# A hybrid mixer kernel: modulation products on TensorE, loads queued later, and other places for stores, gathers and mLSTM fetches

## The chip, the cores and the metric

The kernel runs on one core of a Trainium2 chip. The metric is the device time of one execution in microseconds (us); lower is better. The engines are named as in the profile: PE (TensorE, with PEld for its weight loads), DVE (VectorE), ACT (ScalarE), POOL (GpSimd) and SP, which here only issues DMAs. Each engine works through its own queue in the order of the program.

## The reference

The program computes two transformer blocks over 512 tokens of width 1024, all in float32. The change touches the first half of the first block, the mixer, and the adaptive modulation beside it:

```python
mod = c_act @ ada_w + ada_b                          # one row of 6 x 1024, from silu(c)
hn = rmsnorm(x) * (1 + sc1) + sh1
proj = hn @ w_in                                     # 1024 -> 6208 columns
a_qkv, a_z, a_gates, b_qk, b_v, b_o, b_gates, merge = split(proj)
# branch a: gated delta rule, 8 heads, chunks of 64 tokens, both directions
sol = triangular_solve(lower + I, [v*beta, k*beta*exp(g)])
for c in chunks:  v_new = u_c - w_c @ S;  S = S * cd + kd_c.T @ v_new
# branch b: mLSTM, 8 heads, both directions, weights exp(log_d - m)
y = sigmoid(gate_a) * (o_a @ w_branch_a) + sigmoid(gate_b) * (h_b @ w_branch_b)
x = x + gt1 * (y @ w_out)
```

Behind it come a mixture of 32 experts, and a second block, run as two layers of attention and feed-forward. Each of the three modulations (`ada0`, `ada1`, `ada2`) is one row vector times a 1024 x 6144 matrix, and each weight is used once.

## The kernel before

Activations lie feature-major, 128 features by 512 tokens a tile, split into a high and a low part (`hi`, `lo`), so that a product of weights and activations is three matmuls (`mm3`): high by high, high by low, low by high. Weights come as *units*. A raw block of 1024 x 256 (1 MB, tile `raw`, four buffers) is loaded over the SP queue (`_load`); each unit takes half of it, ACT rounds it to `whi` (L196), POOL subtracts to get `wlo` (L205), and 24 matmuls into a PSUM bank `pd` follow. A unit of the token-major kind (`tm`) does the same with the operands swapped.

The order is written by hand. `unit` first calls `_ahead`, which issues the splits of the next two units; `_loads` issues a new load whenever fewer than four raw blocks are held. Before the change `_loads` also runs after each split in `_ahead` and in `done` for a block used unsplit. This order decides what stands behind what on the queue of SP, which issues the loads of weights, the stores of projected tiles (`later`, one tile behind), the gathers of the delta rule and the reloads.

The modulation unit (`ada`, L457) takes a raw block of 1024 x 256 whole: ACT multiplies four of its eight 128-row slices by `c` in place, DVE multiplies and adds the other four into `adacc`, POOL adds the four of ACT and then the two sums, and two matmuls against a column of ones (`pa<-ones,adacc`) add up the 128 partitions. 24 such units run inside the mixer, 16 more in the first attention layer, 24 in the first feed-forward part (there on DVE alone). The opening of the kernel has another form, `ada_first`: eight matmuls `pada<-wa,crep`, each with 32 equal weight columns, four of them side by side on the array, and then two against `wmean`.

In the mixer two generators run against each other. The main one is the delta rule for four heads (`gdn`, twice) and then the mLSTM; the other, `fill`, is the projection of w_in (`gdn_proj`, `spill_tm`, `spill_fm`), with a modulation unit woven in after every 8.4 credits of work (two pieces at 4.2 each), and the branch product `branch_a` behind it. `drive` takes from `fill` as many credits as the main generator yields; a tile of `pd` is 5.2 credits. So the yields set how much projection is placed between two steps of the delta rule, on every queue.

In `gdn` the steps that matter here are, in order: products `pG`, `M` and `E` on DVE; `M` stored to DRAM (`md`, ACT's queue) and gathered back as `L` by eight DMAs on SP; `Rk` and `kd` on DVE; 31 steps of forward substitution on DVE (`stmp<-L,Tm`, `Tm<-Tm,stmp`), the *solver*; results to DRAM (`yd`, `xd`) and gathered back as `Xc` and `Y` by twelve DMAs; then `pQ`, `pY`, `pw`, `pu`, and a scan over eight chunks (`pv`, `pS`, each answered by DVE).

In the mLSTM a step (head pair f, key block a) needs a tile `rowt`, read from DRAM (`mdram`) and spread over 128 partitions (ACT's queue), masked by POOL (L1399), raised to exp by ACT (`weights`), multiplied on DVE with the scores `pqk`, and used in the matmuls `pm`. After four steps `mlstm_out` normalises, gates with `og` (loaded there, on SP) and transposes (`pht`).

Of the kernel before, what the change touches and what calls it, by code (L numbers as in the profile page):

```python
# [21 lines left out]
P = 128  # L22
# [153 lines left out]
class Build:  # L176
    def __init__(self, tc, I, O, order=None):
        self.tc, self.nc, self.I, self.O = tc, tc.nc, I, O
        self.orders_in = order
        self.orders = {}  # L180
        self.curset = None
        self.uid = 0
        self.lead_ps = {}
        self.pending = None
# [143 lines left out]
    def unit(self, key, sel):  # L328

        i = len(self.order)  # L330
# [27 lines left out]
    def _ahead(self, i):  # L358
        self._loads()
        while self.nsplit < len(self.order_in) and sum(s[0] != "raw" for _, s in self.order_in[i + 1:self.nsplit + 1]) <= self.w_ahead:  # L360
# [12 lines left out]
            self._loads()  # L373
# [83 lines left out]
    def ada(self, w, c, bias, out, groups, eng=None):  # L457
# [3 lines left out]
        for g in groups:  # L461
# [31 lines left out]
            self.tt(out[:, s], ps[:, 0:16], bias[:, s], OP.add)  # L493

# [425 lines left out]
    def gdn_proj(self, g, cv=None, dram=None):  # L920

        for c in range(3):
# [52 lines left out]
    def gdn(self, g, mx, qk, v, Y, Tm, z_d, o_d, side=None, decay=None):  # L975
# [52 lines left out]
        for d in range(2):  # L1028
            for half in range(2):
                for par in range(2):  # L1030
                    p0 = 64 * d + 32 * half + 16 * par
                    s0 = 64 * par + 32 * half
                    dst = (Lr if d == 0 else Lt)[p0:p0 + 16]
                    self.dma("sync", dst, md[s0:s0 + 32, d, :, 32 * half:32 * half + 32].rearrange("r q c -> q r c"))
# [8 lines left out]
        for d in range(2):  # L1043
# [3 lines left out]
            yield 5.0  # L1047
        nc.vector.tensor_copy(Lt[0:64], Lr[0:64, ::-1, ::-1])
        tmp = mx.tile([P, 256], F32, tag="stmp", name="stmp")
        for j in range(31):  # L1050
# [5 lines left out]
            if j % 4 == 3:  # L1056
                yield 2.6
# [190 lines left out]
        yield 5.0  # L1248
        for f in range(2):
# [128 lines left out]
    def mlstm(self, mp, qk, v_d, o_d, oh, ol):  # L1378
# [5 lines left out]
        rowt = {}  # L1384

        def fetch(i):
            if i < len(steps):
                f, a = steps[i]
                t = rowt[i] = mp.tile([P, 2, 640], F32, tag="rowt", bufs=5, name="rowt")
                self.dma("scalar", t, self.mdram[2 * f:2 * f + 2, a, :].partition_broadcast(P))  # L1390

        def weights(i):
            if i < len(steps):
                f, a = steps[i]
                t, n = rowt[i], T - P * a
                for d in range(2):
                    dg = t[:, :, T:] if d else t[:, :, 0:P]
                    sg = -1 if d else 1
                    nc.gpsimd.affine_select(dg, dg, pattern=[[0, 2], [sg, P]], compare_op=OP.is_ge, fill=NEG, base=0, channel_multiplier=-sg)  # L1399
                for hh in range(2):  # L1400
                    for d, r in ((0, t[:, hh, 0:n]), (1, t[:, hh, n:])):
# [1403 lines left out]
```

## Time and profile before

| | |
|---|---|
| median of 3 runs | 2731.18 us (2724.32 to 2737.99) |
| the profiled execution | 2728.39 us, its span 2726.6 us |
| PE busy over the span | 2490.4 us (91%) |
| DVE, ACT, POOL busy | 1524.1, 929.5, 957.9 us |
| granted clock of PE, mean | 0.952 of full speed |
| opening | 0 to 62 us |
| gates and the first projection | 62 to 110 us |
| delta rule, heads 0 to 3, and heads 4 to 7 | 110 to 305, and 305 to 484 us |
| mLSTM | 484 to 632 us |
| merge, output product | 632 to about 790 us |

The stages are told from the tiles: `E` of the first group starts at 110 us, the transposes of the second begin at 329, `va` is loaded at 486.5, `pht` of the last head pair ends at 632. In the later stages (expert mixture, two layers) PE is busy nearly throughout. The chain of work that ended last begins at 1103 us and so says nothing of the mixer; there the waits of PE, taken by stage, are read instead. A granted clock between two levels (1.2 and 2.4 GHz, 0.5 and 1.0 in the rows) is a mean over a stretch.

### The profile page before, as it was taken

The numbers are of one execution on the slowest core, as the hardware profiler recorded it, in microseconds if no ns is written. First come the engines' busy times: TensorE is split into PE (matmuls) and PEld (weight loads), VectorE is DVE, ScalarE is ACT, GpSimd is POOL, SyncE is SP. The second block draws the span as 40 slices with busy tenths as digits, with TensorE's granted clock in tenths as the row PEclk, the third lists the DMA queues.
The fourth block names the chain that finished last, engine by engine and source line by source line (L and its number), as shares of the span: only waits on it lengthen the run. The fifth ranks groups of instructions, "written<-read, shape, count | busy, mean of one in ns | idle before, by whom it ended". The sixth has DMA issues, their size and how long they took to land.

```text
span 2726.6 us, 35040 instructions
## 1 busy us (share of the span) xinstructions
PE 2490.4 (91%) x13618; PEld 1843.4 (68%) x13618; DVE 1524.1 (56%) x2483; ACT 929.5 (34%) x1534; POOL 957.9 (35%) x652
## 2 busy tenths in 40 slices
PE   7888888787969999889999999999999999999999
PEld 4676776566634444557777877878757777888887
DVE  4896595354446645564455488884454345452523
ACT  3434233444222211333444432323332344442432
POOL 1454454332320000443553333444332343344443
PEclk8989898788979999999999999999999999999999
DMA  9356465534389974432446146552331225232321
GB/s 264 93 187 180 150 183 179 203 108 136 102 325 357 391 301 146 135 124 93 146 148 201 63 154 201 170 192 89 102 93 47 85 82 189 78 108 80 106 93 62
DMA packets 332299, 419.07 MB, mean 154 GB/s; under 512 B 33608, under 2 KB 275760, under 8 KB 323680
## 3 DMA queue, kind: packets, MB, share of 16 engines
q1 hardware_dynamic: 312848, 377.12, 41.8%
q10 hardware_dynamic: 14624, 25.28, 2.7%
q0 software_dynamic: 4656, 14.35, 1.6%
q8 instruction: 113, 1.85, 0.3%
q14 instruction: 58, 0.48, 0.1%
HBM read 387.66 MB, written 33.23 MB: 154 GB/s over the span
## 4 chain that ended last, share of the span: by engine, by line
PE 45%; DVE 6%; issue 3%; POOL 2%; ACT 2%; DMA 1%; ACTq 0%; POOLq 0%; DVEq 0%
PE pd L199 36%; PE psc L199 2%; DVE adacc L214 2%; PE tm L199 2%; POOL wlo L205 2%; PE ptot L199 1%; DMA raw<-in_w_up 1%; DVE cv L214 1%; PE po L199 1%; DVE h L214 1%; PE prr L199 1%; PE pc L199 1%; PE pz L199 1%; PE pso L199 1%; PE pst L199 1%
## 5 line engine op out<-in xcount | busy, mean ns | idle before, releaser
L205 POOL TENSOR_TENSOR wlo<-raw,whi 128x1024 fp32r<-128x1024 f32 (+3 forms) x317 | 720.6, 2279 | 1219.3 <-ACT whi L196 1069.6
L199 PE MATMUL pd<-h,whi 128*128 128x512 f32 (+1 forms) x3440 | 1098.6, 401 | 32.9 <-DVE stg L214 6.3
L199 PEld LDWEIGHTS pd<-h,whi 128*128 128x128 f32 x3440 | 646.4, 193 | 191.0 <-issue 27.1
L199 PE MATMUL pd<-h,wlo 128*128 128x512 f32 (+1 forms) x1720 | 675.9, 393 | 21.9 <-POOL wlo L205 21.9
L196 ACT ACTIVATE whi<-raw 128x1024 fp32r<-128x1024 f32 (+3 forms) x319 | 313.9, 993 | 260.4 <-PE pd L199 117.2
L199 PEld LDWEIGHTS pd<-h,wlo 128*128 128x128 f32 x1720 | 331.4, 193 | 94.4 <-POOL wlo L205 26.2
L199 PE MATMUL pd<-fyh,whi 128*128 128x512 f32 (+1 forms) x546 | 204.7, 375 | 9.3 <-ACT whi L196 5.3
L214 DVE SCALAR_TENSOR_TENSOR cv<-pd,vec,cv 128x511 f32<-128x511 f32 (+1 forms) x176 | 131.8, 749 | 143.8 <-ACT cv L196 138.3
L199 PE MATMUL pd<-fyh,wlo 128*128 128x512 f32 (+1 forms) x546 | 201.8, 370 | 5.5 <-POOL wlo L205 5.5
L214 DVE SCALAR_TENSOR_TENSOR adacc<-raw,cs,adacc 128x256 f32<-128x256 f32 x288 | 201.5, 700 | 9.4
L199 PE MATMUL pd<-fyl,whi 128*128 128x512 f32 (+1 forms) x546 | 200.8, 368 | 0.2 <-DVE fyl L205 0.2
L214 DVE SCALAR_TENSOR_TENSOR xTl<-pd,mod,xTl 128x512 f32<-128x512 f32 (+1 forms) x73 | 49.4, 683 | 188.5 <-PE pd L199 188.5
L199 PE MATMUL pgB<-gu,xt 128*64 128x512 f32 (+1 forms) x304 | 143.1, 608 | 0.3 <-PEq L1981 0.3
L199 PE MATMUL pgA<-gu,xt 128*64 128x512 f32 (+1 forms) x304 | 143.2, 608 | 0.0
L199 PE MATMUL tm<-whi,h 128*128 128x256 f32 x640 | 130.7, 297 | 8.3 <-ACT whi L196 7.9
L199 PEld LDWEIGHTS pd<-fyh,whi 128*128 128x128 f32 x546 | 104.6, 192 | 40.1 <-ACT whi L196 10.4
L199 PEld LDWEIGHTS pd<-fyh,wlo 128*128 128x128 f32 x546 | 104.4, 191 | 24.3 <-POOL wlo L205 7.5
L199 PEld LDWEIGHTS pd<-fyl,whi 128*128 128x128 f32 x546 | 104.7, 192 | 16.8 <-DVE fyl L205 0.7
L199 PEld LDWEIGHTS tm<-whi,h 128*128 128x128 f32 x640 | 107.2, 200 | 9.6 <-ACT whi L196 8.2
L199 PE MATMUL tm<-wlo,h 128*128 128x256 f32 x320 | 93.9, 293 | 7.7 <-POOL wlo L205 7.6
L196 ACT ACTIVATE cv<-pd,vec 128x512 f32<-128x512 f32 x88 | 68.2, 775 | 94.5 <-PE pd L199 93.9
L214 DVE SCALAR_TENSOR_TENSOR xT<-pb,mod,xT 128x512 f32<-128x512 f32 x128 | 87.0, 742 | 2.1 <-PE pb L199 1.9
(564 smaller groups left out, 3366.9 us busy)
## 6 DMA issues: line engine op xcount, KB each, us to landing
raw<-in_ada SPq DMA_DIRECT2D x64, 1024.0 KB, 5.4
raw<-in_w_in SPq DMA_DIRECT2D x54, 1024.0 KB, 6.7
raw<-in_w_up SPq DMA_DIRECT2D x44, 1024.0 KB, 4.9
gu<-in_wg SPq DMA_DIRECT2D x30, 1024.0 KB, 8.7
gu<-in_wu SPq DMA_DIRECT2D x30, 1024.0 KB, 7.0
dn<-in_wd SPq DMA_DIRECT2D x59, 512.0 KB, 9.7
raw<-in_w_dn SPq DMA_DIRECT2D x16, 1024.0 KB, 5.1
raw<-in_wo SPq DMA_DIRECT2D x12, 1024.0 KB
```

What stands on the lines that cost most here:

```text
L196: return self.nc.scalar.activation(out, in_, func, **kw)
L199: return self.nc.tensor.matmul(out, lhsT, rhs, start=start, stop=stop)
L205: return (eng or self.nc.vector).tensor_tensor(out, a, b, op=op)
L214: return (eng or self.nc.vector).scalar_tensor_tensor(out, a, s, b, op0=op0, op1=op1)
```

## The change

1. **Modulation products.** The 24 units inside the mixer use a new generator `ada_mm`: eight matmuls `pada<-raw,cs` on the raw block, with a column of `c` repeated 32 times as weights, in four column groups; ACT copies the result to `adacc`; two matmuls against `wmean` one unit later. DVE's, ACT's and POOL's passes over the block go. A unit yields 1.2 credits, where the old one yielded none, and comes after every 6.0 credits. The units of the later stages stay as they are.
2. **Later loads.** `_loads` is called at the head of `_ahead` alone, no longer after a split or in `done`. This holds for the whole program.
3. **Stores.** `later` keeps two tiles back, not one; `gdn` flushes them before its last transposes.
4. **Delta rule.** The eight gathers of `L` are issued after the first `Rk`, `kd` and a yield, no longer before them. The solver yields 3.9 credits every four steps, not 2.6. The projection of z comes before the last third of the second `gdn_proj`.
5. **mLSTM.** `rowt` is fetched on SP, four steps ahead instead of three, with the first (and every sixth) in a buffer of its own. The first one is fetched, masked and raised to exp inside the scan of the second `gdn`. `og` is loaded one step before it is used, into two buffers. `oa` is no longer loaded whole on ACT's queue: `branch_in` loads its quarters on SP, two at the start of the mLSTM and two when the first are split.

```diff
     def _ahead(self, i):
...
             self.nsplit += 1
-            self._loads()
...
     def done(self, u):
...
                 del self.raws[key]
-                self._loads()
...
+    def ada_mm(self, w, c, bias, out, groups):
+        for g in groups:
+            pcol = self.ps.tile([P, T], F32, tag="a", bufs=self.ps_a, name="pa")
+            pend = None
+            for j in range(9):
+                if j < 8:
+                    u = self.unit((w, 0, KD, 2048 * g + 256 * j, 256), ("raw",))
+                    ps = self.pc("pada")
+                    for k in range(KD):
+                        q = 32 * (k % 4)
+                        self.mm(ps[q:q + 32, 0:256], c[:, k:k + 1].to_broadcast([P, 32]), u[1][:, k, :], k < 4, k >= 4)
+                    self.done(u)
+                if pend is not None:
+                    for i in range(2):
+                        self.mm(pcol[:, 2 * j - 2 + i:2 * j - 1 + i], pend[:, i * P:(i + 1) * P], self.wmean)
+                if j < 8:
+                    pend = self.gp.tile([P, 256], F32, tag="adacc", bufs=2, name="adacc")
+                    self.act(pend, ps[:, 0:256], AF.Copy)
+                    yield 1.2
...
             self.tt(Tm[:, j + 1:, 0:w], Tm[:, j + 1:, 0:w], tv, OP.subtract)
             if j % 4 == 3:
-                yield 2.6
+                yield 3.9
...
+    def mlstm_fetch(self, t, f, a):
+        self.dma("sync", t, self.mdram[2 * f:2 * f + 2, a, :].partition_broadcast(P))
...
-            fetch(i + 3)
+            fetch(i + 4)
             weights(i + 2)
...
+                if a == 2:
+                    og[f] = mp.tile([P, 4, P], F32, tag="og", bufs=2, name="og")
+                    self.dma("sync", og[f], o_d[:, :, P * f:P * f + P])
...
     def later(self, out=None, in_=None):
...
+        if out is not None:
+            self.pending.append((out, in_))
+        while len(self.pending) > (2 if out is not None else 0):
+            self.dma("sync", *self.pending.pop(0))
...
-        ada = self.chain(ada0((1, 2)), self.ada("ada1", c2, self.vc("ada_b1"), mod1, (0,), nc.gpsimd))
+        ada = self.chain(self.ada_mm("ada0", c1, self.vc("ada_b0"), mod0, (1, 2)), self.ada_mm("ada1", c2, self.vc("ada_b1"), mod1, (0,)))
...
-                    self.gdn_proj(1, None, cv_d), self.mark("g1"), self.spill_tm("w_in", 1536, 2, z_d),
+                    self.gdn_proj(1, None, cv_d, (0, 1)), self.spill_tm("w_in", 1536, 2, z_d), self.gdn_proj(1, None, cv_d, (2,)), self.mark("g1"),
```

What stands in a row on PE at the first modulation units, in the first delta group. Before, a unit shows there only as the two matmuls against ones:

```order
L199 MATMUL pd<-h_95,wlo 128x512
L199 MATMUL pG<-gqk_472 64x64 x32
L199 MATMUL pa<-ones,adacc 128x1 x2
L199 MATMUL pd<-h_96,whi 128x512
L199 MATMUL pd<-h_104,whi 128x512
L199 MATMUL pd<-h_96,wlo 128x512
```

After, with the same names (`pl` is the norm of the heads, `cs` the column of c):

```order
L199 MATMUL pl_923<-sq,const_gmask 128x512
L199 MATMUL pada<-raw,cs_146 32x256 x8
L199 MATMUL pa<-wmean,adacc 128x1 x2
L199 MATMUL pd<-h_98,whi 128x512
L199 MATMUL pd<-h_106,whi 128x512
L199 MATMUL pd<-h_98,wlo 128x512
```

Eight matmuls have come in between two projection steps; the two that follow belong to the unit before.

On POOL from the clearing of `Tm` to the end of the first solver, before (the group of three `wlo` is the one that PE waits for at 198 us):

```order
L1039 MEMSET Tm 128x32
L205 TENSOR_TENSOR raw<-raw 128x512
L205 TENSOR_TENSOR adacc<-adacc,raw 128x256 x2
L205 TENSOR_TENSOR wlo<-raw,whi 128x1024 x3
L205 TENSOR_TENSOR raw<-raw 128x512
L205 TENSOR_TENSOR adacc<-adacc,raw 128x256 x2
L205 TENSOR_TENSOR wlo<-raw,whi 128x1024
```

and after, from the same clearing to the scan:

```order
L1053 MEMSET Tm 128x1024
L1054 MEMSET Tm 128x32
L205 TENSOR_TENSOR wlo<-raw,whi 128x1024 x10
L1178 MEMSET S 128x256
L205 TENSOR_TENSOR zg<-zg,rows 128x1024
```

The additions of the modulation have left POOL's queue; only the subtractions for `wlo` are left in this stretch.

On SP at the start of the mLSTM, before (`rowt` and `oa` are on ACT's queue there):

```order
L217 DMA raw<-in_w_in 128x8x256
L217 DMA raw<-in_wa 128x4x256
L217 DMA va<-v_d 128x520 x4
L217 DMA row_ml_g<-in_rows 128x512
L217 DMA mg_d<-stg 128x512
```

and after, from the reload of the mLSTM's q and k in the scan on:

```order
L217 DMA mqk_4038<-qk_d 128x512 x2
L217 DMA rowt<-mdram 128x2x640
L217 DMA mg_d<-stg 128x512 x2
L217 DMA raw<-in_wa 128x4x256
L217 DMA mg_d<-stg 128x512 x3
L217 DMA raw<-in_wa 128x4x256
L217 DMA va<-v_d 128x520
L217 DMA rowt<-mdram 128x2x640
L217 DMA va<-v_d 128x520
L217 DMA rowt<-mdram 128x2x640
```

The first `rowt` has moved ahead of the loads of `wa` and `va`, into the scan, and the next ones alternate with `va` on the same queue.

## Rows read from the trace of the kernel before

**Rows 1.** Busy time by stretch (start:end, length, each engine, clock, DMA share, GB/s)
```profile
110.00:484.00 374.00, 307.35 (x3548) 258.00 (x3548) 273.09 (x444) 135.88 (x225) 176.72 (x121) 0.91 0.56 170
140.00:225.00 85.00, 65.42 (x543) 56.91 (x540) 81.23 (x128) 23.77 (x41) 44.70 (x30) 0.88 0.57 169
343.00:412.00 69.00, 56.65 (x288) 47.83 (x286) 65.93 (x101) 20.07 (x34) 35.82 (x25) 0.95 0.64 183
484.00:632.00 148.00, 112.92 (x545) 83.60 (x544) 63.82 (x156) 69.72 (x143) 47.10 (x59) 0.79 0.44 146
```

**Rows 2.** Waits of PE, 110 to 484 us: us in total, times, longest
```profile
PE pd L199 <- POOL wlo L205: 9.2, 1, 9.2
PE pl L199 <- ACT sq L196: 8.5, 2, 5.1
PE tm L199 <- ACT whi L196: 7.9, 2, 6.8
PE tm L199 <- POOL wlo L205: 7.6, 4, 2.0
PE pd L199 <- DVE stg L214: 6.3, 1, 6.3
...
PE pd L199 <- DVE stmp L205: 3.4, 1, 3.4
```

**Rows 3.** Groups by form, 110 to 570 us: count, busy us, mean ns, idle before
```profile
L214 DVE SCALAR_TENSOR_TENSOR adacc<-raw,cs,adacc 128x256 f32<-128x256 f32 x72 | 48.9, 679 | 2.6
L196 ACT ACTIVATE raw<-raw,cs 128x256 f32<-128x256 f32 x96 | 40.7, 495 | 3.8 <-DVE adacc L210 3.8
L205 POOL TENSOR_TENSOR adacc<-adacc,raw 128x256 f32<-128x256 f32 x48 | 40.0, 833 | 54.6 <-DVE adacc L214 51.7
L205 POOL TENSOR_TENSOR raw<-raw 128x512 f32<-128x512 f32 x24 | 34.7, 1445 | 2.1 <-ACT raw L196 2.1
```

**Rows 4.** PE in order of time, opening: start, us, what (two records a matmul)
```profile
43.17 1.92 PE L199 MATMUL pada<-wa,crep 128*32 128x256 f32 x16
...
47.76 1.07 PE L199 MATMUL pada<-wa,crep 128*32 128x256 f32 x16
48.76 0.61 PE L199 MATMUL pa<-wmean,adacc 128*128 128x1 f32 x4
```

**Rows 5.** POOL in order of time, end of the first solver
```profile
193.77 1.56 POOL L205 TENSOR_TENSOR adacc<-adacc,raw 128x256 f32<-128x256 f32 x2 [11.26 <-DVE adacc L214]
195.29 4.96 POOL L205 TENSOR_TENSOR wlo<-raw,whi 128x1024 fp32r<-128x1024 f32 x2
```

**Rows 6.** Start of the mLSTM: ACT's DMA queue, POOL, PE and ACT in order of time
```profile
492.48 1.51 ACTq L217 DMA_DIRECT2D rowt<-mdram  x3
500.84 0.77 POOL L1399 TENSOR_SCALAR_AFFINE_SELECT rowt<-rowt 128x256 f32<-128x256 f32 x2 [14.99 <-DMA rowt<-mdram]
502.98 1.33 PE L199 MATMUL pm<-va,rowt 128*128 128x65 f32 x5 [13.30 <-DVE rowt L214]
531.63 0.63 ACT L196 ACTIVATE oe<-og 128x512 f32<-128x512 f32 x1 [5.21 <-DMA og<-o_d]
```

**Rows 7.** Waits of PE, 484 to 632 us
```profile
PE pqk L199 <- DVE rowt L214: 9.3, 3, 3.7
PE pht L202 <- DVE hs L205: 6.2, 1, 6.2
```

**Rows 8.** SP's queue and DVE at the first solver, in order of time
```profile
146.19 5.43 SPq L217 DMA_DIRECT2D L<-md  x8
166.12 0.68 DVE L1048 COPY L<-L 64x1024 f32<-64x1024 f32 x1
```

**Rows 9.** Waits of PE, 1100 to 2726 us
```profile
PE pd L199 <- POOL wlo L205: 16.2, 12, 2.0
```

**Rows 10.** Waits of SP's queue, 110 to 632 us; a load's time to landing
```profile
SPq L217 <- POOL adacc L205: 88.7, 17, 16.4
raw<-in_ada SPq DMA_DIRECT2D x64, 1024.0 KB, 5.4
```

More of the change, by code (lines that the diff above doesn't have):

```diff
@@ L917, in gates, with gdn_proj @@
         yield 1.0
-    def gdn_proj(self, g, cv=None, dram=None):
-        for c in range(3):
+    def gdn_proj(self, g, cv=None, dram=None, parts=range(3)):
+        for c in parts:
             for j in range(2):
@@ L1047, in gdn @@
             yield 5.0
+            for dd in range(2 if d == 0 else 0):
+                for half in range(2):
+                    for par in range(2):
+                        p0 = 64 * dd + 32 * half + 16 * par
+                        s0 = 64 * par + 32 * half
+                        dst = (Lr if dd == 0 else Lt)[p0:p0 + 16]
+                        self.dma("sync", dst, md[s0:s0 + 32, dd, :, 32 * half:32 * half + 32].rearrange("r q c -> q r c"))
         nc.vector.tensor_copy(Lt[0:64], Lr[0:64, ::-1, ::-1])
@@ L1248, in gdn @@
         yield 5.0
+        self.later()
         for f in range(2):
@@ L1409, in mlstm @@
         self.mlg = self.big_row(mp, "ml_g")
-        for i in range(2):
-            weights(i)
-        out = None
+        weights(1)
+        out, og = None, {}
         for i in range(len(steps) + 1):
@@ L1516, in gate_loads, with branch_in, fetch @@
         return get
-    def branch_in(self, oa, hi, lo):
+    def branch_in(self, src, hi, lo, fill):
+        ts = []
+        def fetch(k):
+            if k < 4:
+                ts.append(self.gp.tile([P, T], F32, tag="mt", bufs=2, name="oat"))
+                self.dma("sync", ts[k], src[:, k])
+        for k in range(2):
+            fetch(k)
+        yield from fill
         for k in range(4):
-            self.split(oa[:, k], hi[:, k], lo[:, k])
+            self.split(ts[k], hi[:, k], lo[:, k])
+            fetch(k + 2)
         yield 0.0
@@ L2650, in pre2 @@
                         yield from self.mlstm_pre(g1["ml"], qk_d)
+                        g1["first"] = mb.tile([P, 2, 640], F32, tag="rowt0", name="rowt")
+                        self.mlstm_fetch(g1["first"], 0, 0)
+                        yield 0.0
+                        yield 0.0
+                        self.mlstm_weights(g1["first"], 0, 0)
                     sh = [P, 2, 4, 4, 64]
@@ L2670, in mixer @@
             with tc.tile_pool(name="mp", bufs=1, reuse_waits="tile") as mp:
[L2671 to L2674 removed]
+                fill = self.chain(self.branch_in(oa_d, hi, lo, fill), place(), self.branch_a("wa", (hi[:, 0:4], lo[:, 0:4]), ya, mg_d, mp, 2))
+                fill = self.drive(self.mlstm(mp, mb, g1["first"], qk, v_d, o_d, oh, ol), fill)
                 self.drain(fill)
```

58 lines of the change are left out of this document (22 added, 36 removed).

## The prediction

> **What bounds the kernel now.** I read the table of busy time by stage first, then the waits of PE inside a stage, then the queues of the engine that PE waited for, in order of time. From 110 to 484 us, the delta rule, PE is busy 307.35 of 374.00 us, so it stands idle for 66.7 [rows 1]. From 484 to 632 us, the mLSTM, it is busy 112.92 of 148.00 and idle for 35.1 [rows 1]. After 1100 us the largest of PE's waits comes to 16.2 us in twelve pieces [rows 9]: there PE's own work is the time. So the kernel as a whole is bound by PE, and the mixer is bound by PE plus about 100 us in which PE waits for somebody. Two places in the mixer have another bound: around the two solvers (140 to 225, 343 to 412 us) DVE is busy 81.23 of 85.00 and 65.93 of 69.00 us [rows 1]. The granted clock of PE is 0.91 over the delta rule and 0.79 over the mLSTM [rows 1], so part of PE's work runs at 1.2 GHz after such waits.
>
> The change takes work from DVE, ACT and POOL and gives PE some. It wins where PE waits for these three, and loses what it adds to PE. The sum is made against the profiled execution, 2728.39 us; the median of the runs shown is 2731.18, which is 2.8 more, and the last step adds that.
>
> **The change part by part.**
>
> *Products on PE: +24.* The same form stands in the opening: eight `pada` matmuls begin at 47.76 and the next product begins at 48.76 us, so a unit costs 1.00 us of PE's time at 2.4 GHz; at 1.2 GHz the same eight took 1.92 us [rows 4]. The two matmuls on the column sums were there before, against ones instead of `wmean`, and cost the same. 24 units make 24 us if PE is otherwise busy. If all ran at 1.2 GHz it would be 46; if half fell into gaps that stay, 12. I take 24, since the gaps that stay by the terms below (66.7 - 18 - 12, a tenth of the stretch) hide little and the clock there is nearer the upper level. The new copy by ACT is beside all this: ACT loses 40.7 us of passes over the block [rows 3] and has 135.88 of 374 us busy [rows 1].
>
> A rule speaks against this part. In the opening the eight column-tiled matmuls of 47.76 last 1.07 us, to 48.83, and the product on the whole array begins at 48.76, before that end [rows 4]. The Trainium skill (TensorEngine Tiling (Array Packing), section Key Properties) says that a change of the tiling mode drains the array, without a figure. By that rule each unit pays two drains, and the 24 us would be more by 48 of them; by the row the drain is inside the 1.00 us or too short to show, and the sum stays.
>
> *What leaves the other queues.* In the mixer the old units hold DVE for 48.9 us in their three later passes, ACT for 40.7, and POOL for 40.0 + 34.7 = 74.7 us [rows 3]. More costly than the work is the order. POOL's additions wait 51.7 us for DVE's sums [rows 3], and the subtractions for `wlo` stand behind them: at 193.77 POOL had been idle for 11.26 us for that reason, and then did several subtractions in a row [rows 5]. That is PE's wait of 9.2 us [rows 2]. With the additions gone, `wlo` waits for ACT's rounding alone.
>
> *Waits for weights: -18.* PE's waits for `wlo` and `whi` in the delta rule come to 9.2 + 7.9 + 7.6 = 24.7 us [rows 2]. The 9.2 goes whole by the reason just told. Of the other 15.5 one wait is 6.8 us for ACT and four are up to 2.0 us for POOL; I keep 7, since the short ones look like a late load followed by ACT and POOL, which stays. Bounds: -9 (only the long one) and -25.
>
> *Waits for DVE and ACT: -12.* Around the solvers PE waits for an evacuation and for the solver itself, 6.3 + 3.4 us, and in the norms 8.5 us for ACT's squares [rows 2], 18.2 together. DVE loses 48.9 us there and elsewhere, and the z tiles, which need one copy each instead of four DVE passes, now lie in the first solver. The solver yields half as much again, so PE has more to do in it. I take 12; the bounds are -4, if DVE stays the bound around the solver because more projection now runs beside it, and -18. The scan's waits of PE for DVE are a dependence and stay.
>
> *Start of the mLSTM: -10.* The three row fetches were issued at 492.48, POOL began on the first at 500.84 and PE at 502.98, after 13.30 us of waiting [rows 6]. Now the first row is ready before the stage starts, and the next three are issued with `va`, without `oa` beside them. The second step still needs its row about 8 us after issue (492.48 to 500.84), of which PE can fill some with the first step. I keep 3 of the 13.3. Bounds -5 and -13.
>
> *The output gate: -5.* ACT waited 5.21 us for `og` [rows 6] with the exponentials of later steps queued behind; PE's three waits for `rowt` later in the stage are 9.3 us together [rows 7]. With `og` loaded a step ahead two of the three should go. The last wait, 6.2 us for `hs` at the end [rows 7], is a chain through DVE, ACT and POOL with little beside it, and stays. Bounds 0 and -9.
>
> *Clock: -14.* From the rows, 0.91 over 374 us means 67 us at 1.2 GHz, and 0.79 over 148 us means 62 us [rows 1]. About half of each is idle time, which costs nothing twice; work in the rest runs at half speed, so some 32 us are lost. With about half of the waits gone I take back 14. Bounds 0 and -26.
>
> *Gathers and fetches that come later: +7.* The eight gathers of `L` were issued from 146.19 on for 5.43 us and DVE used them at 166.12 [rows 8], some 14 us after the last issue. Now they are issued behind the first `Rk` and `kd`, and DVE arrives earlier. +3, between 0 and 10. The last two quarters of `oa` are fetched only when the first are split: a landing of about 5 us as for a load [rows 10], partly hidden; +2, between 0 and 6. In the later stages the loads move one store back on SP; what PE waits there for weights is small [rows 9]; +2, between 0 and 8, if that wait grows by half. The stores kept back cost nothing while the buffer's next user comes a whole tile later; without that cover each costs its landing.
>
> Sum: 24 - 18 - 12 - 10 - 5 - 14 + 7 = -28. 2728.39 - 28 = 2700; at the level of the median 2731.18 - 28 = **2703 us**. All slow bounds together give 46 - 9 - 4 - 5 + 24 = +52, all fast ones 12 - 25 - 18 - 13 - 9 - 26 = -79; neither set will meet.
>
> **The rivals.**
>
> *PE's own work becomes the whole bound.* The added 24 us stay, the waits for weights give 9, the rest of the delta rule nothing, since freed engines only wait for PE earlier; the mLSTM's 15 and a clock of 6 stay, and 7 are added: 24 - 9 - 15 - 6 + 7 = +1, 2732 us. For it: PE is busy for 82% of that stretch already [rows 1]. Against: the 9.2 and 13.3 us waits have causes that the change removes outright.
>
> *PE waits for the modulation's loads.* A matmul on `raw` stands in PE's queue with everything behind it; before, a late block held DVE, ACT and POOL first. Loads are now issued later in the order and every 6.0 credits instead of 8.4. A landing takes 5.4 us [rows 10]. If each of the 24 units makes PE wait 2 us, that is +48, and the time is 2703 + 48 = 2751: slower. It decides from an average wait of about 1.8 us a unit (28 + 14 = 42 us over 24). Against: SP waited 88.7 us for POOL to release these very blocks [rows 10]; now PE's eight matmuls release them. DMA share is 0.56 [rows 1], which leaves room.
>
> *The whole stall opens.* If the waits fall to their lower bounds and the clock follows: 24 - 25 - 18 - 13 - 9 - 26 + 2 = -65, 2666 us. For it: both solvers are DVE-bound by the rows, and DVE is relieved just there. Against: the chain through the gathers and the scan remains.
>
> **How the numbers follow.** A measurement of this kernel can tell about 0.5% (14 us) from no change, so faster means below 2717 and slower above 2745. The forecast, a gain of 14 to 55 us, has 0.60. The whole stall opening has 0.10, PE's own work as the bound 0.18, the waits for loads (or another new wait of that size) 0.12. So faster 0.70, same 0.18, slower 0.12. The range of 2665 to 2738 leaves out the loads' case, half of the fastest case and the last part of the middle one, about 2 in 10.
>
> **What would show it right or wrong.** In the new profile: `pada` at about 1.0 us a unit, in 24 units between 110 and 400 us; no addition of the modulation on POOL before 1100 us, and no wait of PE for `wlo` above 3 us; DVE busy for less than 0.85 of the time around the solvers; the first `pm` within 5 us of the first scores; PE busy over the delta rule for over 0.87 of a stretch that is shorter by 10 to 30 us. It is wrong if PE shows waits for DMA `raw<-in_ada`, if the solver stretches keep their 85 and 69 us, or if the mLSTM's start waits for its second row as long as it did for the first. After 800 us the two profiles should run alike within 8 us.

## The result, and the profile after

The changed kernel takes 2693.09 us, the median of four runs (2686.67 to 2694.69), against 2727.75 for the kernel before beside it. The ratio is 0.9866, with a 95% interval of 0.9844 to 0.9887: 34.7 us, or 1.3%, faster, where 28 were forecast. The profiled execution of it has a span of 2692.6 us (2694.69 with what lies around it) and a mean granted clock of 0.960, against 0.952.

Where the 34.0 us between the two spans went, by the stages of the two traces: the delta rule ends 16 us earlier after its start at 110 (358 us instead of 374); the mLSTM gives another 17 (131 instead of 148); the stretch from there to the first matmul of the experts (tile `pgA`, at 785.0 before, at 761.4 now) gives 9.4 back; the expert stage to the first attention scores (`psc`) is 6.6 shorter (440.6 and 434.0); the rest is 3.8 shorter (1501.0 and 1497.2).

Busy time by stretch in the kernel after (start:end, length, busy time of PE, PEld, DVE, ACT and POOL, then clock, DMA share, GB/s): the delta rule, the two solver stretches, the mLSTM. These answer [rows 1].

```profile
110.00:468.00 358.00, 320.04 (x3894) 257.51 (x3895) 210.75 (x357) 110.11 (x163) 106.91 (x57) 0.93 0.62 186
137.00:208.00 71.00, 67.97 (x556) 55.63 (x558) 64.41 (x102) 14.89 (x22) 21.78 (x8) 0.98 0.75 220
328.00:403.00 75.00, 66.72 (x588) 56.24 (x583) 52.52 (x82) 13.56 (x19) 22.45 (x11) 0.96 0.72 202
468.00:599.00 131.00, 103.10 (x534) 74.81 (x533) 61.36 (x143) 53.72 (x118) 40.71 (x48) 0.86 0.39 128
```

Over the delta rule PE now stands idle for 38 us instead of 66.7, DVE has 62 us less to do and POOL 70 us less. Around the first solver PE is busy for 0.96 of the time and at a clock of 0.98. Before it was 0.77 and 0.88, with DVE busy for 0.96. The stretches of the second solver (75 us after, 69 before) are not cut at the same events. From the start of the first solver step to that of the last, the two solvers take 35.0 and 37.3 us instead of 42.3 and 45.4.

PE's waits in the kernel after, 110 to 468 us (total, times, longest), which answer [rows 2]:

```profile
PE pl L199 <- ACT sq L196: 10.0, 2, 5.9
PE pQ L199 <- DMA Xc<-xd: 5.6, 1, 5.6
PE pw L199 <- ACT Y L196: 3.6, 1, 3.6
...
PE pa L199 <- DVE mod L214: 3.0, 1, 3.0
PE tm L199 <- POOL wlo L205: 3.0, 2, 2.0
...
PE pd L199 <- DVE stg L1294: 1.5, 1, 1.5
...
PE tm L199 <- ACT whi L196: 0.5, 1, 0.5
```

Of the 24.7 us of waits for weights 3.5 are left. The wait of 6.3 us for an evacuation (`stg` of L214) and that for the solver's `stmp` have gone too; `stg` of L1294 is another one, and was 3.1 us before. The wait for the gathered `Xc` has grown from 1.4 to 5.6.

A modulation unit on PE in the kernel after, in the first solver, in order of time, as [rows 4]:

```profile
154.40 1.07 PE L199 MATMUL pada<-raw,cs 128*32 128x256 f32 x16
155.40 0.61 PE L199 MATMUL pa<-wmean,adacc 128*128 128x1 f32 x4
```

And what is left of it on ACT (a group by form, 110 to 570 us: count, busy us, mean ns, idle before), as [rows 3]:

```profile
L196 ACT ACTIVATE adacc<-pada 128x256 f32<-128x256 f32 x24 | 9.1, 379 | 55.2 <-PE pada L199 55.2
```

The start of the mLSTM in the kernel after, in order of time, as [rows 6]: the first row is fetched and masked 37 and 30 us before the first scores.

```profile
431.90 0.37 SPq L217 DMA_DIRECT2D rowt<-mdram  x1
438.75 0.77 POOL L1410 TENSOR_SCALAR_AFFINE_SELECT rowt<-rowt 128x256 f32<-128x256 f32 x2 [5.57 <-DMA rowt<-mdram]
...
468.39 1.13 PE L199 MATMUL pqk<-mqk 64*128 64x512 f32 x4
...
473.45 2.45 PE L199 MATMUL pm<-va,rowt 128*128 128x65 f32 x20
```

PE's waits in the mLSTM, 468 to 599 us, as [rows 7]:

```profile
PE pht L202 <- DVE hs L205: 9.5, 1, 9.5
PE pqk L199 <- DVE rowt L214: 6.6, 3, 3.5
PE pd L199 <- ACT stg L196: 6.4, 2, 5.2
...
PE pm L199 <- DMA rowt<-mdram: 1.8, 1, 1.8
```

### The profile page after: what moved, and what is told of

The parts are those of the page before. It is cut to its first block, busy times and chain, and to the rows that moved or that the text cites. A ratio compares the mean times of both kernels' runs of the same rounds, so it can differ in the third digit from the quotient of the medians.

```text
span 2692.6 us, 35544 instructions
## 1 busy us (share of the span) xinstructions
PE 2498.7 (93%) x14002; PEld 1840.3 (68%) x14002; DVE 1463.9 (54%) x2387; ACT 895.7 (33%) x1458; POOL 885.1 (33%) x580
## 4 chain that ended last, share of the span: by engine, by line
PE 46%; DVE 7%; issue 3%; ACT 2%; POOL 2%; DMA 1%; POOLq 0%; ACTq 0%; DVEq 0%
PE pd L199 36%; DVE adacc L214 2%; PE psc L199 2%; PE tm L199 2%; POOL wlo L205 1%; PE ptot L199 1%; DMA raw<-in_w_up 1%; DVE cv L214 1%; PE po L199 1%; PE pz L199 1%; PE pc L199 1%; DVE h L214 1%; PE pso L199 1%; PE pst L199 1%; PE prr L199 1%
## 5 line engine op out<-in xcount | busy, mean ns | idle before, releaser
L214 DVE SCALAR_TENSOR_TENSOR cv<-pd,vec,cv 128x511 f32<-128x511 f32 (+1 forms) x176 | 131.8, 749 | 143.2 <-ACT cv L196 137.7
L214 DVE SCALAR_TENSOR_TENSOR adacc<-raw,cs,adacc 128x256 f32<-128x256 f32 x216 | 156.4, 724 | 6.9
L214 DVE SCALAR_TENSOR_TENSOR xTl<-pd,mod,xTl 128x512 f32<-128x512 f32 (+1 forms) x73 | 49.4, 683 | 189.2 <-PE pd L199 189.1
L199 PEld LDWEIGHTS pd<-fyh,wlo 128*128 128x128 f32 x546 | 105.1, 193 | 24.7 <-POOL wlo L205 7.5
L199 PEld LDWEIGHTS pd<-fyl,whi 128*128 128x128 f32 x546 | 105.3, 193 | 16.4
L214 DVE SCALAR_TENSOR_TENSOR xT<-pb,mod,xT 128x512 f32<-128x512 f32 x128 | 86.8, 742 | 1.9 <-PE pb L199 1.9
```

Source lines behind the costliest of these rows:

```text
L199: return self.nc.tensor.matmul(out, lhsT, rhs, start=start, stop=stop)
L214: return (eng or self.nc.vector).scalar_tensor_tensor(out, a, s, b, op0=op0, op1=op1)
```

## The experiments

The prediction added its terms up as if they were independent. The rival theory is that they depend on each other. So four of the five items of the change were made alone on the kernel before, and taken alone out of the changed kernel. The fifth, the stores kept two tiles back, was not tried apart and stands in every run that starts from the changed kernel. The ratio is to the kernel before on the same chip. Beside it stands the start of the first expert matmul of the profiled execution, which ends the mixer. The *routing* below is the first transpose of `xa`, which follows the output product.

| kernel | median, us | ratio (95%) | first expert matmul |
|---|---|---|---|
| before | 2727.75 | 1 | 785.0 |
| changed | 2693.09 | 0.9866 (0.9844 to 0.9887) | 761.4 |
| before + products (b_ada) | 2724.43 | 0.9995 (0.9983 to 1.0007) | 789.6 |
| before + delta-rule moves (b_delta) | 2762.51 | 1.0136 (1.0112 to 1.0159) | 822.4 |
| before + later loads (b_loads) | 2714.62 | 0.9952 (0.9934 to 0.9971) | 776.6 |
| before + mLSTM part (b_mlstm) | 2716.17 | 0.9960 (0.9945 to 0.9974) | 777.2 |
| changed, old modulation units (a_oldada) | 2746.39 | 1.0080 (1.0053 to 1.0108) | 811.5 |
| changed, moves undone (a_nodelta) | 2709.28 | 0.9933 (0.9909 to 0.9957) | 772.5 |
| changed, solver yields 2.6 (a_yield26) | 2715.48 | 0.9949 (0.9931 to 0.9967) | 775.0 |
| changed, early loads (a_loads) | 2728.25 | 0.9997 (0.9977 to 1.0017) | 782.7 |
| changed, old mLSTM (a_nomlstm) | 2699.87 | 0.9897 (0.9878 to 0.9916) | 757.1 |
| changed, products twice (a_twice) | 2703.39 | 0.9913 (0.9890 to 0.9936) | 769.3 |
| changed, late fill (a_last) | 2691.95 | 0.9854 (0.9832 to 0.9875) | 752.6 |
| the same, 3 quarters of oa early (a_last_oa) | 2690.97 | 0.9856 (0.9834 to 0.9879) | 759.4 |

The four parts alone add up to -1 + 37 - 13 - 11 = +12 us (ratio less 1, by 2728); the whole change, with the stores, makes -37. What each is worth inside the changed kernel is the difference of two ratios, by 2728, uncertain by 8 to 10 us each: products 58, later loads 36, moves 18, mLSTM part 8.

**The products, alone and taken out.**

```diff
-        ada = self.chain(ada0((1, 2)), self.ada("ada1", ..., (0,), nc.gpsimd))
+        ada = self.chain(self.ada_mm("ada0", ..., (1, 2)), self.ada_mm("ada1", ..., (0,)))
...
-                    ... self.mark("end")), ada, 4.2)
+                    ... self.mark("end")), ada, 6.0)
```

> The kernel before with the modulation products alone (24 units on PE, woven in after every 6.0 credits); loads, stores, delta rule and mLSTM as before. Theory (what the change wins here is the order on POOL and the work on DVE): PE gets 24 us more, its waits for wlo and whi in the delta rule fall from 24.7 to about 7 us, the waits for DVE and ACT around the solvers by half of the 12 us forecast, since the solver still yields as little as before, and the clock gives back some 6: 24 - 18 - 6 - 6 = -6 us, so 2715 to 2727 against 2728. Rival (PE's own work is the bound): the 24 us stay and only the long wait of 9.2 goes: about +10 us. Second rival (the freed DVE makes the solvers short, and the delta rule is bound by its chain): -15 us or more, with solver stretches shorter by over 8 us each.

Alone it is no gain. The delta rule ends at 456 instead of 484, but less projection was placed beside it, and that stands behind the mLSTM now. The two stretches from the last `pht` to the routing, kernel before and then b_ada:

```profile
631.20:699.80 68.60, 58.74 (x218) 44.59 (x216) 29.13 (x34) 20.83 (x31) 21.22 (x9) 0.87 0.48 158
```

```profile
596.00:704.30 108.30, 90.78 (x349) 69.92 (x348) 34.35 (x41) 33.35 (x48) 33.17 (x14) 0.91 0.43 139
```

PE's work there has grown by 32 us. From 110 us to the routing PE is busy for 16.4 us more and idle for 12 less, so what the waits give, the added work takes. That comes near the first rival of the prediction in the time, but not in its words: the delta rule did gain 28 us, and PE is still idle for 100 of 594 us. The theory's -6 and the rival's +10 lie on either side of the measured -1.4 (interval -5 to +2).

The opposite edit on the changed kernel:

> The changed kernel with the modulation's units undone: the old form with its passes on DVE, ACT and POOL, woven in after every 4.2 credits; all else as changed. Theory (the parts depend on each other: the moves of the delta rule put more projection beside the solvers, which pays only if DVE is freed of the modulation): the sum of the single parts, +37 for the moves, -11 for the loads, -10 for the mLSTM, so about 2742 us, slower than before, with DVE busy for over 0.93 of the solver stretches. Rival (the parts add up): the change without its products is worth -34 + 1 = -33, so about 2694 us, like the changed kernel. Second rival (the later loads free POOL's queue also for the old units, and the moves are then harmless): about 2710 us.

The theory's 2742 was close. Busy time of a_oldada around the first solver:

```profile
140.00:240.00 100.00, 79.06 (x590) 67.47 (x590) 86.30 (x129) 25.34 (x44) 46.09 (x31) 0.90 0.59 170
```

DVE is at 0.86 of this stretch, short of the announced 0.93. Over the solver's steps alone (163.5 to 218.2 us) it is busy for 52.1 of 54.7 us, 0.95, so they are bound by DVE. The first solver's results are stored 26 us later (`xd` at 219.8, against 194.2 in the changed kernel).

**The moves of the delta rule, alone and undone.**

```diff
             if j % 4 == 3:
-                yield 2.6
+                yield 3.9
```

with the gathers of `L` behind the first `Rk` and `kd` and z ahead of the last third of the second projection, as in the change.

> The kernel before with the moves in the delta rule alone: gathers of L behind the first Rk and kd, the solver yields 3.9 credits instead of 2.6 every four steps, z before the last third of the second projection. Theory (DVE is the bound around the solvers, so more projection beside them does not help while DVE and POOL still carry the modulation's sums): between -5 and +5 us, with the solver stretches no shorter than 85 and 69 us. Rival (the solver lacked work for PE, the moves alone fill it): -10 us or more, PE busy for over 0.85 of the stretch of the first solver.

Neither theory: 37 us slower, all of it in the mixer. Busy time of b_delta around the first solver (compare the second line of [rows 1]):

```profile
140.00:240.00 100.00, 82.06 (x669) 70.79 (x668) 91.58 (x140) 28.43 (x49) 48.48 (x31) 0.88 0.61 166
```

PE is busy for 0.82 instead of 0.77 of the time, and DVE has 10 us more to do, in a stretch that is 15 us longer (over the steps alone it is busy for 0.95 of the time, as before). The solver's 31 steps end at 223.5 instead of 209.5 and, in the second group, at 438.8 instead of 404.4. The steps themselves account for 13 of these 34 us (53.4 and 47.7 us instead of 42.3 and 45.4). Elsewhere in the delta rule PE's waits for the evacuation `stg` of L214 have grown from 6.3 to 15.7 us; the rest was not taken apart, nor were the three edits of this run. The projection is then used up inside the mLSTM (the branch product's first gate comes at 562.9), whose PE is busy for 104 us of 150. This is the bound that the prediction named for one term ("if DVE stays the bound around the solver because more projection now runs beside it", -4), and it costs over four times the 8 us that the bound allowed for it. That DVE is the reason is argued from these rows and from the runs below.

> The changed kernel with the moves of the delta rule undone: gathers of L early, 2.6 credits a yield in the solver, z behind the second projection; all else as changed. Theory (with DVE freed, the solvers have room for more projection, and it is the larger yield that uses it): products -1, loads -11, mLSTM -10 give -22, so about 2704 us, some 12 slower than the changed kernel; the delta rule is then shorter than in the changed kernel, and what it leaves of the projection stands behind the mLSTM (the stretch from the last pht to the routing about 100 us against 76). Rival (the moves cost also with the products on PE, as they do alone): 2680 us or less, faster than the changed kernel.

As expected, slower: 18 us by the ratios, to some 9. With the products on PE the same moves gain.

> The changed kernel with 2.6 instead of 3.9 credits every four steps of the solver; gathers and z as changed. Theory (the larger yield is what makes the moves of the delta rule worth 16 us with the products on PE, by placing more projection beside the solvers): about 2707, with over 15 us more between the last pht and the routing. Rival (gathers behind Rk and z beside the solver carry it): within 4 us of the changed kernel.

The yield alone accounts for all of it (23 us by the ratios, to some 8, where the theory had 14). The stretch from the last `pht` to the routing, in the changed kernel and then with 2.6 credits:

```profile
597.50:674.60 77.10, 68.60 (x259) 51.67 (x257) 33.42 (x39) 28.82 (x42) 22.99 (x10) 0.90 0.54 175
```

```profile
591.80:688.60 96.80, 88.98 (x349) 68.38 (x348) 33.27 (x41) 34.10 (x48) 33.51 (x14) 0.93 0.50 161
```

Twenty microseconds of PE's work that fit beside the solvers stand behind the mLSTM otherwise.

One more link joins the products and the moves, and the prediction left it out: the credits. Each of the 24 new units takes 1.2, together 28.8, which at 5.2 a tile is 5.5 tiles of projection that the delta rule no longer places. The larger yield, 1.3 credits more at seven places in each of two solvers, gives back 18.2 credits, or 3.5 tiles of 24 matmuls. The traces show it (records of `pd` in the delta rule; steps of the solvers, from the start of the first to that of the last):

| kernel | `pd` matmuls | first and second solver, us |
|---|---|---|
| before | 588 | 42.3, 45.4 |
| before + products (b_ada) | 462 | 32.7, 31.9 |
| changed, solver yields 2.6 (a_yield26) | 462 | 31.7, 32.0 |
| changed | 552 | 35.0, 37.3 |
| changed, old modulation units (a_oldada) | 672 | 54.5, 50.2 |
| before + delta-rule moves (b_delta) | 675 | 53.4, 47.7 |

Two things follow. The products do free the solvers: before and after, about as much projection stands beside the steps (161 and 160 matmuls before, 169 and 169 now), and they are 7 and 8 us shorter. But the changed kernel's delta rule holds 36 projection matmuls fewer than the one before, not more. Some 90 more make the delta rule 46 us longer without the products (b_delta) and 3 us longer with them (from a_yield26 to the changed kernel). How much of that is owed to freed engines and how much to the smaller number of tiles is not shown: no run keeps the old units and lets them take 1.2 credits.

**The later loads, alone and undone.**

```diff
             self.nsplit += 1
-            self._loads()
...
                 del self.raws[key]
-                self._loads()
```

> The kernel before with the later loads alone (loads are issued at the head of the look-ahead, no longer after a split or a freed block). Theory: +2 us, between 0 and 8, as in the sum: each load goes out one unit's work later, and PE's waits for a landing grow a little in the stages after 800 us. Rival (a load issued later lets stores and gathers pass ahead on SP, which then no longer waits for POOL with a load at the head of its queue): -5 us or more, with SP's waits for the modulation's blocks below half of 88.7 us.

> The changed kernel with the early loads back (after each split and after each freed block). Theory (the later loads help by what passes ahead of them on SP, gathers and stores; the products on PE free their blocks in PE's order, so less waits at the head of that queue): +6 us, about 2699. Rival (the gain of 11 us of the later loads alone came from the old units holding a load at the head of SP's queue for 88 us, which the products have removed): no difference within 3 us. Second rival (the gain is in the stages after 1100 us, where the old units stand in both kernels): +11 us, and half of it after 1000 us.

The later loads alone are 13 us faster; with the early loads put back into the changed kernel it is 36 slower by the ratios, to some 8. In b_loads the rival has the sign and the size, but not its place: SP's waits for the modulation's blocks (`adacc`, 110 to 632 us) fall from 88.7 to 68.3 only, those for `wlo` from 82.8 to 28.7. All three theories of a_loads fall by size. The largest single place (14 of the 21 us up to the experts) is the branch product and the merge. SP, ACT and POOL there in a_loads, in order of time:

```profile
623.06 0.38 SPq L217 DMA_DIRECT2D raw<-in_wb  x1
...
623.53 1.78 SPq L217 DMA_DIRECT2D mg<-mg_d  x2
...
627.29 0.63 ACT L196 ACTIVATE mg<-mg 128x512 f32<-128x512 f32 x1 [6.19 <-DMA mg<-mg_d]
...
627.83 1.04 ACT L196 ACTIVATE whi<-raw 128x1024 fp32r<-128x1024 f32 x1
...
628.95 2.40 POOL L205 TENSOR_TENSOR wlo<-raw,whi 128x1024 fp32r<-128x1024 f32 x1 [5.92 <-ACT whi L196]
...
631.38 0.38 SPq L217 DMA_DIRECT2D raw<-in_wb  x1
```

It is a closed loop. The load of the next block waits on SP for POOL's subtraction on the block just split. The two gates `mg` are queued behind that load. ACT waits for the gate, and its next rounding `whi` is queued behind the gate; POOL waits for the rounding, and SP for POOL. One round takes 631.38 - 623.06 = 8.3 us for a pair of tiles. SP's queue in the changed kernel:

```profile
618.03 0.39 SPq L217 DMA_DIRECT2D raw<-in_wb  x1
620.36 3.04 SPq L217 DMA_DIRECT2D mg<-mg_d  x2
623.49 0.39 SPq L217 DMA_DIRECT2D raw<-in_wb  x1
625.80 3.04 SPq L217 DMA_DIRECT2D mg<-mg_d  x2
628.93 0.39 SPq L217 DMA_DIRECT2D raw<-in_wo  x1
```

A round takes 5.45 us. In a_loads SP waits for POOL's `wlo` 85.5 us between 575 and 700, in seven pieces; in the changed kernel 22.6 between 565 and 675, in two. The kernel before has the same loop, at some 9.7 us a round (loads at 633.59, 643.11 and 653.01), and b_loads shows one round of 5.4 (638.73, 644.17): its stretch from the last `pht` to the routing is 59.4 us against 68.6. Up to the mLSTM's end a_loads is 7.5 us later than the changed kernel; that part was not taken further apart, nor were the 11 us by which its profile is longer behind the first expert matmul.

**The mLSTM part, alone and undone.** The edits of item 5 of the change, whole.

> The kernel before with the mLSTM's part alone: rowt on SP's queue four steps ahead, the first row made ready in the scan, og a step early, oa in quarters. Theory: the start wait of 13.3 us goes but for 3, og gives 5, the clock about 6, the quarters take 2: -19 us, between -10 and -28. Rival (what is won is given back behind the mLSTM, where the branch product waits for quarters of oa and the merge for its last head pair): the last pht is earlier by 15 us or more, but the first merge by less than 8, and the time moves by less than 8 us.

> The changed kernel with the mLSTM's part undone: rowt on ACT's queue three steps ahead, first row made ready at the start, og late, oa whole on ACT's queue. Theory (this part is independent of the others, it gave 10 us alone): about 2703, 10 slower than the changed kernel, with a wait of PE for the first row of 12 us or more. Rival (what it wins at the start is filled by projection anyway now, since more is left over): within 4 us of the changed kernel.

Alone 11 us by the ratio, 7.8 of it before the experts: little more than half of the theory's 19. The rival, that the gain is given back behind the mLSTM, falls: the last `pht` is 8 us earlier, and so are the experts. Taken out of the changed kernel it makes 8 us by the ratios (to some 8), but the mixer of that profile is not longer (757.1 against 761.4). PE waits 12.1 us for the first row, yet the delta rule, in which the first row is not made ready, ends 8 us earlier (460.2 against 468.1), and with `oa` loaded whole the stretch behind the last `pht` is 70.5 us instead of 77.1. So this part's gain on top of the others is small, and is not shown beyond doubt.

**The price of PE's work.**

```diff
-                    for k in range(KD):
+                    for k in 2 * list(range(KD)):
                         q = 32 * (k % 4)
```

> The changed kernel with the eight matmuls of each of its 24 modulation units done twice (the first pass is overwritten). Measures the price of PE work in this place. Theory (PE is the bound, a unit costs about 1.0 us, little of it falls into gaps): +18 to +24 us, about 2714. Rival (what stands idle in the delta rule, 38 us, takes the work): +12 us or less. Second rival (the switch between column groups and the whole array is dear): over +24 us.

A doubled unit in the trace (compare 154.40 above), and PE from 110 us to the routing in a_twice and in the changed kernel:

```profile
155.37 1.93 PE L199 MATMUL pada<-raw,cs 128*32 128x256 f32 x32
157.23 0.61 PE L199 MATMUL pa<-wmean,adacc 128*128 128x1 f32 x4
...
110.00:682.80 572.80, 508.00 (x5050) 392.19 (x5047) 308.08 (x538) 192.20 (x321) 175.47 (x115) 0.93 0.55 169
```

```profile
110.00:674.60 564.60, 490.24 (x4678) 382.69 (x4678) 305.31 (x538) 192.05 (x321) 170.61 (x115) 0.91 0.56 171
```

A second set takes 0.86 us more (157.23 - 155.37 less 1.00), 21 us for 24 units. PE is busy for 17.8 us more, and the stretch is 8.2 longer: idle time falls from 74 to 65, and the clock rises from 0.91 to 0.93. The program is 13 us slower by the ratios, to some 9. So PE's work added here costs about half of its own time, nearer to the rival (12 or less) than to the theory, whose 18 the interval still reaches.

**A version that fills the last wait.**

```diff
         self.tt(hv, hv, og, OP.mult)
-        yield 1.0
+        yield 9.0 if f == 3 else 1.0
         ps = self.pc("pht")
```

> The changed kernel with one number altered: at the last head pair of the mLSTM the step before the transposes yields 9.0 credits instead of 1.0, so that projection still left stands on PE ahead of the last pht. Theory (what is left behind the mLSTM, 68.6 us of PE's work in 77, is bound by PE, and the last wait of 9.5 us for hs can take some of it): the wait goes but for 1 or 2 us and the time falls by 5 to 9 us, to about 2686. Rival (the stretch behind the mLSTM is paced by loads on SP's queue, one pair of tiles in 5.4 us): the wait goes, the first merge is not earlier, the time is the same within 2 us. Second rival (the last pht is held up by the work put ahead of it and the merge with it): slower by 2 us or more.

> As the run with 9.0 credits, and three quarters of oa are fetched at the start of the mLSTM instead of two (the third in a buffer of its own), the fourth when the first is split. Theory (ACT waits 4.9 us for the later quarters and PE 3.8 us for ACT's splits, because the fetches stand behind stores on SP): another 2 to 4 us less than the run with 9.0 credits alone. Rival (the split by ACT and DVE of the first quarters sets the pace, not the loads): no difference within 2 us.

The wait of 9.5 us for `hs` is gone in both, and in a_last the mixer ends 8.8 us earlier (752.6). Yet the time is the same within what was measured: the ratios are 0.9854 and 0.9856, against 0.9866 (0.9844 to 0.9887). By the ratios a_last is 3 us faster than the changed kernel, to some 8, so the theory's 5 to 9 us and the rival's none are both possible, and the price of this wait stays open. In the profile 7.5 of the 8.8 us stand against a longer expert stage (441.5 us instead of 434.0). In a_last this line, PE's wait in the expert stage, is the largest part of it:

```profile
PE pst L202 <- DVE sa L214: 5.1, 1, 5.1
```

In the changed kernel's profile that wait is absent, and in all thirteen others it is there, with 1.9 to 6.0 us. So the changed kernel's profile is the exception, and the longer stage is no effect of this edit. The third quarter of `oa` fetched early shows no further gain, as its rival expected.

## Why the prediction was right, and where it was wrong

The sign and the size hold, in part by luck. Of the forecast -28, the mixer was to give -30 and the later stages +2. The two profiles show -23.6 up to the first expert matmul and -10.4 behind it, so that two errors cancel in part. Of the -10.4, 6.6 lie in the expert stage, where the changed kernel's 434.0 us are the shortest of fourteen profiles (436.8 to 441.6 in the others).

*Products, +24.* The unit costs 1.00 us as forecast, in 24 units from 108 to 374 us. But from 110 to the routing PE's busy time rises by 12.0 us only (478.2 to 490.2), the rest being taken back by the clock (0.88 to 0.91), for which the sum had a term of its own, below. What was too high is the price: a_twice puts that of more such work at about half, since the gaps hide more than a tenth (idle time takes 10 of its 17.8 us). What was left out is that each unit also takes credits, and so moves projection out of the delta rule. By the rule of the Trainium skill on the change of the tiling mode (TensorEngine Tiling (Array Packing), section Key Properties), which the prediction cites, 48 drains were to be added. The unit inside the mixer takes 1.00 us from the first matmul to the next product, as in the opening, so what the drains cost, if anything, is inside the 1.00 us, as the prediction had it.

*Waits for weights, -18.* 24.7 fell to 3.5: -21, for the reason given. The additions have left POOL's queue, and the long waits with them.

*Waits for DVE and ACT, -12.* Of 18.2 us 10.0 are left (`pl` for the squares), so -8. What the term missed is that the products and the larger yield only work together. The two alone give -1 and +37; without the products the rest of the change is 22 us slower than before by the ratio. The step that failed is the addition: the prediction let each edit meet the trace of before, with DVE as the bound around the solvers and 588 projection matmuls in the delta rule, and not the state that the other edits leave.

*Start of the mLSTM, -10, and the output gate, -5.* The wait of 13.3 is gone, and the first `pm` comes 5.1 us behind the first scores. The second row makes PE wait 1.8 instead of the forecast 3. The waits for `rowt` fell by 2.7, not by two of three; `pht` waits 9.5 instead of 6.2, so the output gate's -5 is not seen. With -17 the stage gained what the terms with their share of the clock said, but behind it 9.4 us were given back. That is work: PE's busy time from 599 to the experts is 133.8 us against 123.1 before from 632 on, with 252 projection matmuls up to the routing instead of 210. PE waits 3.8 us at the splits of `oa`, 2.6 of them for the late quarters; the +2 for them was about right.

*Clock, -14.* Over the delta rule 0.91 became 0.93 and over the mLSTM 0.79 became 0.86. Up to the routing PE was given 24 us and shows 12 more, so as far as busy time tells, 12 of the 14 came. These are the same 12 us as under the products.

*Gathers and fetches that come later, +7.* The worst step. The loads cost nothing: they are worth 13 us alone and 36 inside the changed kernel. The prediction looked at what a later load would make PE wait, and not at what stands behind an early one on SP. [rows 10] already showed SP held for 88.7 us at loads that wait for the modulation's blocks. The waits that the later loads cut most are another kind, those for `wlo` (82.8 us before, 28.7 in b_loads). The gathers of `L` came earlier, not later: DVE uses them at 154.4 instead of 166.1, and the products bring that: it is 157.7 with them alone, 168.0 with the moves alone. In the stages from the first scores on, the nine profiles with later loads take 1494 to 1498 us and the five with early loads 1498 to 1502, with means of 1496 and 1499, so about -3 there instead of +2.

*The rivals.* PE waits nowhere for `raw<-in_ada`, so the second is out. The first, PE's own work as the bound, is close to b_ada in the time; with the larger yield the changed kernel, at -34.7, is well clear of that rival's +1. The third asked for -65.

*The announced signs.* PE is busy for 0.89 of a delta rule that is 16 us shorter, and no wait for `wlo` is above 2.0 us. DVE around the solvers is 0.91 and 0.70, against "below 0.85": the first missed, since DVE's work there fell from 81.2 to 64.4 us but the stretch nearly as much, from 85 to 71. The sign on stretches of 85 and 69 us is met by the solvers' steps, 7 and 8 us shorter; the second stretch as cut here, 75 us, does not show it. The first `pm` comes at 5.1 us, a hair beyond the 5. After 800 us the profiles differ by 10 us, not by 8 at most; 6.6 of that is the expert stage.

*Open.* Whether the expert stage of the changed kernel is 6.6 us shorter in most executions, or was in this one, was not settled; that no other profile is so short speaks for this one. The stores that are kept two tiles back were not tried apart, and the share of the credits in what joins products and moves stays open.

## What to carry to other kernels

Terms taken from one trace add up only while the bound stays where it is, and while each edit leaves the other work in its place; when one edit frees an engine or takes credits, and another fills or gives them, weigh them as a pair and count what is placed where. Before costing a load that is issued later, look at what is queued behind it while it waits for its buffer: a load that waits for the very work which needs what stands behind it makes a loop, and its price is the length of a round. An added piece of work on the busiest engine costs what the remaining gaps and the clock don't take back, here about half (with a wide interval).

## What the runs showed of the hardware that was not expected

An operation of DVE on two SBUF operands that begins beside a subtraction on POOL lasts until POOL is done. The changed kernel, in order of time, at the end of the mLSTM:

```profile
593.26 2.34 POOL L205 TENSOR_TENSOR wlo<-raw,whi 128x1024 fp32r<-128x1024 f32 x1 [1.53 <-ACT whi L196]
593.57 2.58 DVE L205 TENSOR_TENSOR hs<-hs,nr 128x512 f32<-128x512 f32 x1
...
596.25 0.69 DVE L205 TENSOR_TENSOR hs<-hs,og 128x512 f32<-128x512 f32 x1
```

The first product ends at 596.15, 0.55 us after POOL at 595.60; the next one, of the same size with POOL free, takes 0.69. The Trainium skill (SBUF — State Buffer, section on the two separate sides) says that the two engines hold a shared pair of ports by an exclusive lock for a whole instruction, where the operation of DVE has two SBUF inputs and that of POOL reads SBUF; the trace agrees. Beside the solver it is the same: in the changed kernel a `wlo` begins at 157.49 and lasts 2.40 us, the step `Tm<-Tm,stmp` begins at 157.52 and lasts 2.44, and the next, larger one takes 0.22. So each `wlo` beside the solver's chain can delay a step of it by some 2 us. The 62 operations of the steps took 35.9 us of DVE in the first solver before, and 29.7 in the changed kernel, where POOL was busy for 12.4 us beside them instead of 19.3.

The expert stage starts with an indirect gather of `xg` while the DMA share is 1.0. The second gather's use in the changed kernel, and then in a_twice, with the wait of PE that follows there:

```profile
785.49 1.15 ACT L196 ACTIVATE xg<-xg,tab 128x1024 f32<-128x1024 f32 x1 [10.67 <-DMA xg<-xa_d,ids]
```

```profile
798.98 1.15 ACT L196 ACTIVATE xg<-xg,tab 128x1024 f32<-128x1024 f32 x1 [17.84 <-DMA xg<-xa_d,ids]
...
802.11 0.67 PE L202 MATMUL pst<-const_ident,sa 128*128 128x128 f32 x2 [5.64 <-DVE sa L214]
```

Over the fourteen profiles this wait of PE is 0 in the changed kernel's and between 1.9 and 6.0 us in the others, and the stage takes 434.0 us and between 436.8 and 441.6. Why the gather lands late in some of them was not tried; its place among the experts' weights in a saturated DMA is an argument, not a finding.
